# Summing two modulation rows over partitions by accumulating and doubling transfers

## The chip, the cores and the metric

The kernel runs on one core of a Trainium2 chip. TensorE (PE) multiplies matrices, VectorE (DVE) and ScalarE (ACT) do elementwise work, GpSimd (POOL) and SyncE (SP) mostly issue transfers (DMAs), and 16 DMA engines move the data. On-chip memory (SBUF) and the matrix accumulators (PSUM) have 128 partitions. The metric is the time of one execution in microseconds (us), lower is better; the kernel before takes 1791.58 us, the median of three runs (1788.38, 1791.58, 1792.2).

## The reference

One decoder layer, x of 256 tokens by 2048 channels in float32, modulated by a conditioning vector c of 2048. What matters here:

```python
mod = (silu(c) @ w_ada + b_ada).reshape(B, 6, 1, D)
sh1, sc1, gt1, sh2, sc2, gt2 = (mod[:, j] for j in range(6))
h = rmsnorm(x, g_mix) * (1 + sc1) + sh1
z = h @ w_in                       # three token mixers and three gates come from z
...
merged = (sigmoid(gm) * (out_m @ w_branch[0]) + sigmoid(gd) * (out_d @ w_branch[1])
          + sigmoid(gs) * (out_s @ w_branch[2]))
x = x + gt1 * (merged @ w_out)
h = rmsnorm(x, g_ffn) * (1 + sc2) + sh2
hid = h @ w_up
gate = causal_dwconv(hid[..., :D_FF], w_ffconv)
x = x + gt2 * ((silu(gate) * hid[..., D_FF:]) @ w_down)
```

The two gates gt1 and gt2 are rows of 2048 numbers. In the kernel tokens lie on partitions where a gate is used, so each gate is wanted as a tile of 128 partitions that all hold the same row.

## The kernel before

**Products.** All large products go through `gemm` (line 350). It walks the inner dimension in steps of four 128-row tiles. For each step `weights` (line 330) loads 1 MB from SP into one of three `raw` buffers, ACT casts two tiles at a time to the rounded type (`hi`, line 342), DVE subtracts to get the remainder (`lo`, line 344; four buffers each for `hi` and `lo`), and PE multiplies hi and lo parts (lines 377 and 391) into PSUM banks; three banks carry the tag `gp`.

**Modulation rows beside the products.** The rows of `mod` are not made on PE. `ada_late` (line 286) makes 512 columns, called a group here, in eight steps: each loads 512 KB of `w_ada` from SP into one of three `ada` buffers (line 293) and DVE multiplies by a column of silu(c) and adds into an accumulator `acc` (two instructions a step, lines 222 and 224). At the end `acc` holds 128 partial sums, one on each partition. There are two `acc` buffers.

**Gate rows.** `ada_row` (line 308) does four such groups. After each it loads 512 numbers of the bias from POOL (`br`, line 315), adds them to partition 0 of `acc` (line 316), splits `acc` into hi and lo parts (ACT line 418, DVE line 419), multiplies both by a 128x128 matrix of ones (two PE instructions into `pr`, line 321), which leaves the sum over partitions on every partition, and copies it to the row (ACT, line 322).

**Order.** The steps stand as a Python generator in the queue `ada`. `tick()` (line 209) is called after each four-tile step of a product and advances that queue by `rates["ada"]` steps on average: the source weaves the modulation steps among the products with these rates. `issue_after` holds an instruction behind another one on the same engine. A planner then sets each engine's order when the program is built: it walks a timing model of its own and issues what that model has ready. On the chip every queue runs in that order and an instruction that waits holds up those behind it.

**Where the two rows stand.** The row for `gt1` is appended at line 962 ahead of `branch(0, ...)`, at 1.4 steps per tick; what is left is drained at line 967. Then POOL loads the two halves of x again (`x2`, line 970), and the product with `w_out` uses the row in line 981. The row for `gt2` is appended at line 1045, in the second chunk of the up product, at 0.8 steps per tick; it is first used in line 1083, after the first down product.

Of the kernel before, what the change touches and what calls it, by code (L numbers as in the profile page):

```python
# [10 lines left out]
F32 = mybir.dt.float32  # L11
F32R = mybir.dt.float32r
AF = mybir.ActivationFunctionType
ALU = mybir.AluOpType
# [3 lines left out]
P = 128  # L18
# [21 lines left out]
def kernel(  # L40
# [6 lines left out]
    nc = tc.nc  # L47
# [7 lines left out]
    adap = ctx.enter_context(tc.tile_pool(name="adap", bufs=3))  # L55
# [5 lines left out]
    adaps = ctx.enter_context(tc.tile_pool(name="adaps", bufs=1, space=PSUM))  # L61

    def slot(i, name):
        n = NT * MH * (MDH + 1) + 8 if i == 2 else 2048
        return slots.tile([P, n], F32, tag=f"s{i}", name=name)
# [13 lines left out]
    V, A, T = nc.vector, nc.scalar, nc.tensor  # L79
# [6 lines left out]
    ones_r = const.tile([P, P], F32R, name="ones_r")  # L86
# [105 lines left out]
    ada = deque()  # L192
# [14 lines left out]
    rates = {"ada": 0.0, "side": 1.0}  # L207
# [9 lines left out]
    def ada_mac(accs, raw, kt0, nk):  # L217
        for k in range(nk):
# [4 lines left out]
            else:  # L223
                state["mac"] = V.scalar_tensor_tensor(acc, raw[:, k, :], ccol[:, kt:kt + 1], acc, ALU.mult, ALU.add)  # L224

    def partition_sums(acc):

        pm = adaps.tile([P, 512], F32, tag="adaps", name="pm")
        for k in range(4):
            T.transpose(pm[:, k * P:(k + 1) * P], acc[:, k * P:(k + 1) * P], ident)  # L230
        sums = tmp.tile([P, 4], F32, tag="sums", name="sums")
        V.tensor_reduce(sums, pm.rearrange("p (k f) -> p k f", k=4), AX.X, ALU.add)
        return sums
# [52 lines left out]
    def ada_late(comp, g):  # L286

        acc = adap.tile([P, 512], F32, tag="acc", name="acc", bufs=2)
        c0 = comp * D + g * 512
        for q in range(8):  # L290
            raw = adap.tile([P, 2, 512], F32, tag="ada", name="araw")
            with tc.issue_after(state["load"].ins):
                nc.sync.dma_start(raw, w_ada[q * 256:(q + 1) * 256, c0:c0 + 512].rearrange("(k p) f -> p k f", p=P))
            with tc.issue_after(state["split"].ins):
                ada_mac([acc], raw, 2 * q, 2)
            yield acc

    def ada_columns(comp, bcol, dst, gcol=None):
        for g in range(4):
            for acc in ada_late(comp, g):  # L300
                yield
            pm = partition_sums(acc)
            ks = slice(4 * g, 4 * g + 4)
            V.tensor_tensor(dst[:, ks], pm[:, 0:4], bcol[:, ks], ALU.add)
            if gcol is not None:
                V.tensor_tensor(dst[:, ks], dst[:, ks], gcol[:, ks], ALU.mult)

    def ada_row(comp, dst):

        for g in range(4):  # L310
            for acc in ada_late(comp, g):
                yield
            br = adap.tile([P, 2, 512], F32, tag="ada", name="br")[:, 0, :]
            c0 = comp * D + g * 512
            nc.gpsimd.dma_start(br[0:1, :], b_ada[0:1, c0:c0 + 512])
            V.tensor_tensor(acc[0:1, :], acc[0:1, :], br[0:1, :], ALU.add)
            pr = adaps.tile([P, 512], F32, tag="adaps", name="pr")
            parts = adap.tile([P, 2, 512], F32R, tag="ada", name="parts")
            split(parts[:, 0, :], parts[:, 1, :], acc)
            for i in range(2):  # L320
                T.matmul(pr, lhsT=ones_r, rhs=parts[:, i, :], start=i == 0, stop=i == 1)  # L321
            A.copy(dst[:, g * 512:(g + 1) * 512], pr)

    a1 = const.tile([P, KD], F32, name="a1")
    b1 = const.tile([P, KD], F32, name="b1")
# [90 lines left out]
    def split(hi, lo, src):  # L416

        A.copy(hi, src)
        return V.tensor_tensor(lo, src, hi.bitcast(F32), ALU.subtract)
# [438 lines left out]
    def branch(bi, col_g, act, order):  # L858
        for ch in range(4):
            if order == 0:  # L860
                sg = mg_of(ch)
            else:
                sg = [wide("sg"), wide("sg")]
                gates(col_g, ch, sg)
            accb = gemm("T", act, w_branch[bi], 0, ch * 512, 512, 0, KM)
            for tt in range(NT):
                d = mg_of(ch)[tt]
                V.tensor_tensor(sg[tt], accb[tt], sg[tt], ALU.mult)
                if order:
                    V.tensor_tensor(d, d, sg[tt], ALU.add)  # L870
            if order == 2:
                for k2 in range(2):
                    pb = bank("pmg")
                    for tt in range(NT):
                        for j in range(2):
                            k = 2 * k2 + j
                            T.transpose(pb[:, j * S + tt * P:j * S + (tt + 1) * P], mg_of(ch)[tt][:, k * P:(k + 1) * P],
                                        ident)
                    h0 = (ch % 2) * 4 + 2 * k2
                    split(mgh[ch // 2][:, h0:h0 + 2, :], mgl[ch // 2][:, h0:h0 + 2, :],  # L880
                          pb.rearrange("p (a t) -> p a t", a=2))
            tick()
# [31 lines left out]
    for ch in range(2):  # L914
        acc = gemm("T", hact, w_in, 0, C_MO + ch * 512, 512, 0, KD)
# [6 lines left out]
    for ch in range(2):  # L922
        acc = gemm("T", hact, w_in, 0, C_MV + ch * 512, 512, 0, KD)
# [5 lines left out]
    for t, col0, f0 in ((mqT, C_MQ, 0), (mkT, C_MK, 8)):  # L929
        for ch in range(2):  # L930
            acc = gemm("H", h1act, w_in, 0, col0 + ch * 512, 512, 0, KD)
# [28 lines left out]
    mgl = [slots.tile([P, 8, S], F32R, tag=f"s{i}", name=f"mgl{i}") for i in (6, 7)]  # L960
    gt1 = slot(0, "gt1")
    ada.append(ada_row(2, gt1))
    rates["ada"] = 1.4
    branch(0, C_GM, mlstm.out, 2)


# [9 lines left out]
    for ch in range(4):  # L976
        acc = gemm("T", mact, w_out, 0, ch * 512, 512, 0, KD)
# [57 lines left out]


    gt2 = slot(8, "gt2")
    rates["ada"] = 0.8
    NCH = DFF // 512
    for half, (c0, c1) in enumerate(((0, 6), (6, NCH))):  # L1040
        ath = [slots.tile([P, 8, S], F32R, tag=f"s{i}", name=f"ath{i}") for i in (0, 3, 4)]
        atl = [slots.tile([P, 8, S], F32R, tag=f"s{i}", name=f"atl{i}") for i in (5, 6, 7)]
        for ch in range(c0, c1):
            if ch == 1:
                ada.append(ada_row(5, gt2))
# [19 lines left out]
            i, j0 = (ch - c0) // 2, ((ch - c0) % 2) * 4  # L1065
# [12 lines left out]
        for n in range(4):  # L1078
            acc = gemm("T", act, w_down, c0 * 512, n * 512, 512, 0, 4 * (c1 - c0))
# [37 lines left out]
```

## Time and profile before

| | before |
|---|---|
| median of three runs | 1791.58 us |
| the profiled execution, its own time | 1787.35 us |
| span of that execution | 1785.6 us |
| granted PE clock | 0.999 of full |
| busy: PE / DVE / ACT / POOL | 99% / 73% / 53% / 1% |
| products with ones of the two rows (line 321) | 16 |
| transfers issued from POOL for the two rows (line 315) | 8 |

A profile page has the share of each engine, the span in 40 slices, the chain of work that ended last (followed back from the last instruction to what released each step), and groups of instructions with busy time, mean duration and what ended the idle time before them. Further views used below list one engine's instructions in order of time, who waited for whom, the busy times in chosen windows, and the DMAs with the time from issue to landing. In a window row the columns after the window are its length, then busy us (and instructions) of PE, PE's weight loads, DVE, ACT and POOL, then the granted PE clock, the share of the DMA engines that was busy, and GB/s. PE's busy share counts overlapping instructions once, so how fast PE runs is better read from the distance between starts.

### The profile page before, as it was taken

How to read it: one execution, taken by the hardware profiler on the slowest of the kernel's cores; microseconds unless marked ns; L12 is line 12 of the kernel's file. 1: busy time of each engine (PE TensorE's matmuls, PEld its weight loads, DVE VectorE, ACT ScalarE, POOL GpSimd, SP SyncE). 2: the span in 40 equal slices, each digit the busy share in tenths (PEclk: the TensorE clock that was granted, in tenths of full speed). 3: DMA queues.
4: the chain of work that ended last, by engine and by line, in shares of the span. 5: the costliest groups of instructions: out<-in, count | busy, mean ns of one | idle time of the engine just before them, and what ended most of it. 6: DMA issues, size and time to landing. Idle time of an engine off the chain costs nothing.

```text
span 1785.6 us, 23761 instructions
## 1 busy us (share of the span) xinstructions
PE 1762.2 (99%) x9168; PEld 1512.5 (85%) x9168; DVE 1302.4 (73%) x1734; ACT 951.9 (53%) x1338; POOL 16.4 (1%) x44
## 2 busy tenths in 40 slices
PE   7899999999999999999999999999999999999998
PEld 6898999888878887888888888888888888888887
DVE  6887646878888778777996577888875556666654
ACT  6667655666565556544444555555553345555432
POOL 2000000000000000000000000000000000000000
PEclk9999999999999999999999999999999999999999
DMA  9999855776777567778896547777755555555563
GB/s 338 346 330 313 289 179 178 266 244 242 248 238 259 200 216 251 240 261 294 308 323 216 181 166 259 253 251 267 268 204 198 193 189 189 189 189 189 189 214 117
DMA packets 219731, 423.33 MB, mean 237 GB/s; under 512 B 9027, under 2 KB 31675, under 8 KB 219105
## 3 DMA queue, kind: packets, MB, share of 16 engines
q1 hardware_dynamic: 217328, 417.44, 68.8%
q0 software_dynamic: 1008, 2.23, 0.4%
q10 hardware_dynamic: 1280, 2.14, 0.3%
q8 instruction: 72, 1.18, 0.3%
q14 instruction: 43, 0.34, 0.1%
HBM read 419.68 MB, written 2.10 MB: 236 GB/s over the span
## 4 chain that ended last, share of the span: by engine, by line
PE 95%; ACT 2%; DMA 1%; DVE 1%; issue 1%; SPq 0%; ACTq 0%
PE gp L391 55%; PE acch L377 32%; PE kept L396 2%; PE gp L396 2%; DMA raw<-in_w_in_dram 1%; ACT hi L342 1%; PE psc L679 0%; PE pm L240 0%; DMA x<-in_x_dram 0%; DVE quads L224 0%; PE spin L186 0%; ACT x L444 0%; PE pr L321 0%; PE pxt L453 0%; PE ptf L739 0%
## 5 line engine op out<-in xcount | busy, mean ns | idle before, releaser
L344 DVE TENSOR_TENSOR lo<-raw,hi 128x1024 fp32r<-128x1024 f32 (+1 forms) x608 | 724.0, 1208 | 363.4 <-ACT hi L342 327.1
L342 ACT CAST hi<-raw 128x1024 fp32r<-128x1024 f32 (+1 forms) x608 | 617.6, 1039 | 552.4 <-PE gp L391 353.6
L391 PE MATMUL gp<-hi,h 128*128 128x512 f32 (+1 forms) x1600 | 411.4, 387 | 7.0 <-ACT hi L342 5.7
L377 PE MATMUL acch<-h,hi 128*128 128x512 f32 x1664 | 403.3, 392 | 0.2 <-DVE h L1032 0.2
L377 PEld LDWEIGHTS acch<-h,hi 128*128 128x128 f32 x1664 | 303.6, 188 | 58.0 <-DVE h L1032 1.1
L391 PEld LDWEIGHTS gp<-hi,h 128*128 128x128 f32 x1600 | 295.7, 188 | 60.7 <-ACT hi L342 8.8
L391 PE MATMUL gp<-lo,h 128*128 128x512 f32 (+1 forms) x800 | 227.5, 384 | 0.0
L377 PEld LDWEIGHTS acch<-h,lo 128*128 128x128 f32 x1664 | 217.8, 191 | 11.1
L377 PE MATMUL acch<-h,lo 128*128 128x256 f32 x1664 | 221.3, 283 | 0.0
L224 DVE SCALAR_TENSOR_TENSOR acc<-araw,ccol,acc 128x512 f32<-128x512 f32 x240 | 179.3, 748 | 6.0 <-DMA araw<-in_w_ada_dram 4.3
L391 PEld LDWEIGHTS gp<-lo,h 128*128 128x128 f32 x800 | 149.7, 188 | 26.2 <-DVE lo L344 0.8
L391 PE MATMUL gp<-hi,atl 128*128 128x512 f32 x352 | 137.2, 390 | 0.0
L391 PE MATMUL gp<-hi,ath 128*128 128x512 f32 x352 | 136.9, 389 | 0.0
L391 PE MATMUL gp<-lo,ath 128*128 128x512 f32 x352 | 105.9, 390 | 0.0
L391 PEld LDWEIGHTS gp<-hi,atl 128*128 128x128 f32 x352 | 66.1, 188 | 13.7
L391 PEld LDWEIGHTS gp<-hi,ath 128*128 128x128 f32 x352 | 66.1, 188 | 13.7
L391 PEld LDWEIGHTS gp<-lo,ath 128*128 128x128 f32 x352 | 66.1, 188 | 13.6
L224 DVE SCALAR_TENSOR_TENSOR quads<-raw,ccol,quads 128x1024 f32<-128x1024 f32 x45 | 57.7, 1282 | 2.8 <-DMA raw<-in_w_ada_dram 2.2
L391 PE MATMUL gp<-hi,mgl 128*128 128x512 f32 x128 | 50.4, 394 | 0.0
L391 PE MATMUL gp<-hi,mgh 128*128 128x512 f32 x128 | 50.0, 392 | 0.0
L1057 DVE SCALAR_TENSOR_TENSOR y<-gsum,cols,y 128x255 f32<-128x255 f32 (+1 forms) x88 | 41.4, 479 | 3.7 <-ACT y L1055 3.5
L391 PE MATMUL gp<-lo,mgh 128*128 128x512 f32 x128 | 38.3, 391 | 0.0
(365 smaller groups left out, 1601.2 us busy)
## 6 DMA issues: line engine op xcount, KB each, us to landing
raw<-in_w_in_dram SPq DMA_DIRECT2D x98, 1024.0 KB, 5.1
raw<-in_w_up_dram SPq DMA_DIRECT2D x88, 1024.0 KB, 5.1
araw<-in_w_ada_dram SPq DMA_DIRECT2D x128, 512.0 KB, 5.9
raw<-in_w_down_dram SPq DMA_DIRECT2D x44, 1024.0 KB, 5.1
raw<-in_w_ada_dram SPq DMA_DIRECT2D x62, 512.0 KB, 5.9
raw<-in_w_branch_dram SPq DMA_DIRECT2D x24, 1024.0 KB, 5.1
raw<-in_w_in_dram SPq DMA_DIRECT2D x25, 880.0 KB, 5.0
raw<-in_w_out_dram SPq DMA_DIRECT2D x16, 1024.0 KB, 5.0
```

Source lines behind the costliest of these rows:

```text
L224: state["mac"] = V.scalar_tensor_tensor(acc, raw[:, k, :], ccol[:, kt:kt + 1], acc, ALU.mult, ALU.add)
L342: A.copy(hi[:, :, :n], raw[:, k0:k0 + 2, :n])
L344: state["split"] = V.tensor_tensor(lo[:, :, :n], raw[:, k0:k0 + 2, :n], hi[:, :, :n].bitcast(F32), ALU.subtract)
L377: T.matmul(acc[t][:, 0:m], lhsT=w[k // 2][:, k % 2, sl], rhs=ah(s0 + k)[:, 0:m], start=start, stop=s0 + k == kt1 - 1 and w is (wh if flip ...
L391: T.matmul(o, lhsT=a(s0 + k)[:, sl], rhs=wk[:, :n], **kw)
L396: T.matmul(o, lhsT=wk[:, sl], rhs=a(s0 + k), **kw)
L1057: V.scalar_tensor_tensor(yf[:, sft:S], src[:, 0:S - sft], wc(2 - sft), yf[:, sft:S], ALU.mult, ALU.add)
```

## The change

In `ada_row` the products with ones go. In each group `fold(acc)` sums over partitions in place: seven transfers from POOL, each adding the upper half of what is left onto the lower half (64, 32, 16, 8, 4, 2 and 1 partitions of 2 KB). Then the bias is added to partition 0 as before, and one more transfer copies the 2 KB to partition 0 of the row. After the four groups seven transfers double the row (1, 2, 4, ... 64 partitions of 8 KB) until all 128 partitions hold it. The steps per tick go from 1.4 to 2.0 for the first row and from 0.8 to 1.1 for the second.

```diff
+    def fold(acc):
+
+        n = P // 2
+        while n:
+            nc.gpsimd.dma_start(acc[0:n], acc[n:2 * n], accum_op=ALU.add)
+            n //= 2
+
...
         for g in range(4):
             for acc in ada_late(comp, g):
                 yield
+            fold(acc)
             br = adap.tile([P, 2, 512], F32, tag="ada", name="br")[:, 0, :]
             c0 = comp * D + g * 512
             nc.gpsimd.dma_start(br[0:1, :], b_ada[0:1, c0:c0 + 512])
             V.tensor_tensor(acc[0:1, :], acc[0:1, :], br[0:1, :], ALU.add)
-            pr = adaps.tile([P, 512], F32, tag="adaps", name="pr")
-            parts = adap.tile([P, 2, 512], F32R, tag="ada", name="parts")
-            split(parts[:, 0, :], parts[:, 1, :], acc)
-            for i in range(2):
-                T.matmul(pr, lhsT=ones_r, rhs=parts[:, i, :], start=i == 0, stop=i == 1)
-            A.copy(dst[:, g * 512:(g + 1) * 512], pr)
+            nc.gpsimd.dma_start(dst[0:1, g * 512:(g + 1) * 512], acc[0:1, :])
+        n = 1
+        while n < P:
+            nc.gpsimd.dma_start(dst[n:2 * n, :], dst[0:n, :])
+            n *= 2
...
     ada.append(ada_row(2, gt1))
-    rates["ada"] = 1.4
+    rates["ada"] = 2.0
     branch(0, C_GM, mlstm.out, 2)
...
     gt2 = slot(8, "gt2")
-    rates["ada"] = 0.8
+    rates["ada"] = 1.1
```

## The prediction

> **What bounds the kernel now.** I read the page's shares and chain first, then the stage of the first row (813 to 973 us).
>
> ```profile
> span 1785.6 us, 23761 instructions
> PE 1762.2 (99%) x9168; PEld 1512.5 (85%) x9168; DVE 1302.4 (73%) x1734; ACT 951.9 (53%) x1338; POOL 16.4 (1%) x44
> PE 95%; ACT 2%; DMA 1%; DVE 1%; issue 1%; SPq 0%; ACTq 0%
> ```
>
> PE carries 95% of the chain that ended last: an instruction fewer on PE is time saved as long as the others feed it. For the window 800 to 980 us that chain is PE alone:
>
> ```profile
> by line: PE gp L391 96.7%; PE pmg L877 1.9%; PE pr L321 1.0%; PE px L1005 0.2%; PE pm L230 0.2%
> ```
>
> How near the others are shows in the windows:
>
> ```profile
> 872.00:904.00 32.00, 32.00 (x146) 26.45 (x145) 29.05 (x36) 14.05 (x17) 0.48 (x1) 1.00 0.93 324
> 940.00:960.00 20.00, 20.00 (x94) 16.55 (x93) 13.20 (x14) 9.21 (x12) 0.57 (x1) 1.00 0.70 246
> 1140.00:1180.00 40.00, 40.00 (x234) 35.44 (x233) 34.43 (x48) 20.32 (x29) 0.00 (x0) 1.00 0.79 273
> ```
>
> While the first row is made, DVE is busy 91% and the DMA engines 93%; once it is done they fall to 66% and 70%. The second row's stage (third line) has 86% and 79%.
>
> **What goes from PE.** The distance between starts gives PE's pace:
>
> ```profile
> 855.31 0.62 PE L321 MATMUL pr<-parts,ones_r 128*128 128x512 f32 x2
> 855.77 1.09 PE L391 MATMUL gp<-hi,h 128*128 128x512 f32 x4
> L321 PE MATMUL pr<-parts,ones_r x16: 392/394/396, 855.3 to 1319.3; 128*128 128x512 f32 x16
> ```
>
> Two products take 0.46 us of PE's order, so 0.23 each (the 394 ns of one overlap its neighbours). Sixteen: 16 x 0.23 = 3.7 us, all on the chain. First term: -3.7.
>
> The splits (lines 418 and 419) and the copy (322) of eight groups leave ACT and DVE, neither of which is on this chain: nothing by themselves.
>
> **How long the new path is.** No row shows a transfer from on-chip memory to itself, nor one that adds. The nearest are these (KB each, median us from issue to landing; below, POOL's issue time and the spread of landings):
>
> ```profile
> rows<-in_c_dram SPq DMA_DIRECT2D x1, 8.0 KB, 1.6
> x2a<-in_x_dram POOLq DMA_DIRECT2D x1, 1024.0 KB, 5.0
> br<-in_b_ada_dram POOLq DMA_DIRECT2D x8, 2.0 KB, 4.3
> L315 POOL DMA_DIRECT2D br<-in_b_ada_dram x8: 484/484/512, 836.9 to 1294.1; - x8
> DMA to landing us min/median/max: 3.2/4.3/6.7
> ```
>
> Call one step of the new chains s. It lies between 1.6 (SP, almost idle engines) and 6.7. I take 3.2, the shortest `br`: same queue, same busy engines, but the source lies on chip; its end for the range is 4.3 and beyond. The Trainium skill, "DMA: Bandwidth & Descriptors" (Anatomy of one DMA), fits 2.0 us plus bytes over 436 GB/s for a POOL transfer, which would be an estimate of 2.0 to 3.2 us a step here and make every wait below vanish. This trace's 2 KB took 3.2 to 6.7, so the rows decide.
>
> A group's chain c is seven folds, the bias add and the copy to the row: 8s plus one add.
>
> ```profile
> L316 DVE TENSOR_TENSOR acc<-acc,br x8: 673/679/681, 842.2 to 1311.2; 1x512 f32<-1x512 f32 x8
> ```
>
> c = 8s + 0.7. The doubling d is seven steps that grow to 512 KB; at most 0.7 each above a small one (5.0 against 4.3), I take half: d = 7s + 2.5.
>
> **When the first row is there.** Its first multiply, two of its bias loads (one group apart), and its deadline:
>
> ```profile
> 813.21 0.48 DVE L222 TENSOR_SCALAR acc<-araw,ccol 128x512 f32<-128x512 f32 x1
> 902.05 0.48 POOL L315 DMA_DIRECT2D br<-in_b_ada_dram  x1 [31.61 <-PE gp L391]
> 934.03 0.48 POOL L315 DMA_DIRECT2D br<-in_b_ada_dram  x1 [31.50 <-DVE acc L224]
> L981 DVE TENSOR_TENSOR t<-gp,gt x8: 682/691/692, 972.4 to 1043.4; 128x512 f32<-128x512 f32 x8
> ```
>
> A group of eight steps at 1.4 a tick takes 32 us, so a tick is 32 x 1.4 / 8 = 5.6 us; at 2.0 a group takes 22.5. The first ends near 813.2 + 22.5 = 835.7. The later ones go slower, since `br` keeps one of the three `ada` buffers until its add, which now waits for the folds, 7s. With two buffers left and
>
> ```profile
> araw<-in_w_ada_dram SPq DMA_DIRECT2D x128, 512.0 KB, 5.9
> L224 DVE SCALAR_TENSOR_TENSOR acc<-araw,ccol,acc 128x512 f32<-128x512 f32 x240 | 179.3, 748 | 6.0 <-DMA araw<-in_w_ada_dram 4.3
> ```
>
> a step takes (5.9 + 1.5) / 2 = 3.7 us instead of 2.8. At s = 3.2 that holds for 23 us, some 6 steps, and the other two take 5 us: a group of 28. (The two `acc` buffers ask for less: c = 26.3.) The multiplies end at 835.7 + 3 x 28 = 920, the last chain at 946, the row at 971, just ahead of 972.4. By the same working s = 2.5 gives 957 and s = 4.3 gives 835.7 + 3 x 29.6 + 35.1 + 32.6 = 992. The point from which it is late is about s = 3.3. I cost it at nothing; without that cover each us late is one for PE.
>
> POOL's order: behind the new transfers in the source stand the two x loads.
>
> ```profile
> 739.45 0.58 POOL L970 DMA_DIRECT2D x2b<-in_x_dram  x1 [179.75 <-ACT num L819]
> 952.18 0.57 POOL L970 DMA_DIRECT2D x2a<-in_x_dram  x1 [17.67 <-PE gp L391]
> ```
>
> One is issued before the row begins; the other waits for PE's last use of its place. Behind the last doubling it would be issued at about 968 and land 5.0 later, with the row. Nothing beyond the row's own lateness.
>
> **The second row.** Its first multiply, and its deadline:
>
> ```profile
> 1090.05 0.48 DVE L222 TENSOR_SCALAR acc<-araw,ccol 128x512 f32<-128x512 f32 x1
> L1083 DVE TENSOR_TENSOR t<-gp,gt x16: 681/691/692, 1348.3 to 1780.6; 128x512 f32<-128x512 f32 x16
> ```
>
> With the same tick a group is 8 / 1.1 x 5.6 = 41 us, the multiplies end near 1254, the row at 1257 + 15s = 1305, 43 us early; late only from s = 6.1. Nothing.
>
> **What the higher rate costs.** At 2.0 steps a tick needs 1.05 MB of weights and 1.05 MB of `w_ada`: 2.10 MB in 5.6 us is 374 GB/s. The window of 872 moved 324 at a share of 0.93, so 348 with nothing idle: a tick becomes 6.0 us, short by 0.4 in each of 16 ticks, 6.5 us. DVE needs, from the same window, 29.05 less 16 x 0.75 and the removed split, 16.3 in 5.7 ticks, 2.9 a tick; with four multiply-adds 5.9 against 5.6, short by 5 us in 16 ticks. What covers this:
>
> ```profile
> ACT hi L342 <- PE gp L391: 77.7, 48, 3.4
> ```
>
> From 800 to 980 us ACT waited 48 times for a `hi` buffer that PE frees: conversions run ahead until the four buffers are full, three spare ones of twelve products at 0.23, some 8 us. Both shortfalls fit in, and the shortage of `ada` buffers eases both. In SP's order more `w_ada` loads stand ahead of each weight load, and one that waits for its buffer holds the weights behind it, again under that cover. Bounds 0 (these are waits, no gain) to 6.5; I take +2, since other waits use the cover too.
>
> **The new wait on DVE.** The bias add now stands behind seven folds, and behind it in DVE's order stand the `lo` splits that PE needs. Where the planner put such an add:
>
> ```profile
> 937.38 1.53 DVE L224 SCALAR_TENSOR_TENSOR acc<-araw,ccol,acc 128x512 f32<-128x512 f32 x2
> 940.83 0.68 DVE L316 TENSOR_TENSOR acc<-acc,br 1x512 f32<-1x512 f32 x1 [1.92 <-DMA br<-in_b_ada_dram]
> 941.44 1.21 DVE L344 TENSOR_TENSOR lo<-raw,hi 128x1024 fp32r<-128x1024 f32 x1
> ```
>
> The load issued at 934.03 landed 6.7 later, and DVE stood for 1.92 with a split behind it, so real waits are not foreseen exactly. But the planner does move work: x2b, written after the row in the source, was issued ahead of it. I expect the add late in DVE's order, off by under 1 us a step, 7 us a group, against 8 us of cover, thinner in the first stage. Bounds 0 (a wait gains nothing) to 8 x (7 x 2 - 8) = 48, off by 2 a step (5.2 for the 3.2 taken, inside the rows); I take +3, near the low end, as one `br` wait in eight is the nearest row.
>
> **Sum.** -3.7 + 2 + 3 = +1.3 on the profiled execution's 1787.35 (span 1785.6, 1.75 around it): 1788.65. The median is 4.2 above that execution, which gives 1791.58 + 1.3 = 1793 as runs are timed. A measurement of this kernel tells about 0.2%, 3.6 us, from no change.
>
> **Rivals.** A, the first row is late: line 981 waits for it, and with two of three banks unread PE stops after about 1.4 us of products. From s = 3.3 on; at 3.8 the row is some 10 us late, 9 more than the forecast, 1802; at the median of the `br` loads, 4.3, 20 late, 1812. For it: half of those loads took 4.3 or more, and the forecast has 1 us to spare. Against: their source is HBM. Chance 0.28.
>
> B, the planner takes a fold for shorter than it is by more than 1.2 us. DVE then stands at each of eight adds beyond PE's cover. At 1.7 off, 8 x (12 - 8) = 32 replaces the +3: 1822. For it: the 1.92 above. Against: one wait in eight. Chance 0.16.
>
> C, all is hidden: 1791.6 - 3.7 = 1788, from 3.5 to 5 under before if the pace elsewhere is a little better. For it: PE waits nowhere in 800 to 980 us though DVE and DMA are over 90%. Against: it needs every cover at once. Chance 0.22, of which 0.16 beyond 0.2%.
>
> D, a rule of the chip: each POOL issue waits for the DVE instruction under way, about 0.75 to 1.2 us of a multiply-add or split. That makes s 4.2, the row 18 us late: 1810. Against: eight issues at 484 to 512 ns while DVE was busy about 90%. Chance 0.04. The rule is that of the Trainium skill, "SBUF — State Buffer" (Who interferes with whom): DVE in its two-port modes shuts GpSimd out of the port with which it writes transfer descriptors. The trace does not show it.
>
> **Numbers.** Forecast 0.30, all within 0.2%. Slower: A + B + D = 0.48; same: 0.30 + 0.06 = 0.36; faster 0.16. Cases of both signs hold much, so the forecast's own range stands here: 1789 to 1795. Range: low 1785, C less 3 us for the spread of runs (3.8 before); high 1822, B, which takes in A up to 4.3; left out are worse forms of A and B.
>
> **What would show it.** PE without line 321; the group chains 26 us, from the first fold's issue to the copy's landing; adds (line 316) with DVE idle under 8 us before them and no PE wait behind them; the row landing just ahead of 972 and line 981 waiting for PE. Wrong if line 981 or the adds wait for DMA and PE's starts open behind them, or if steps take 4 us or more.

## The result and the profile after

The changed kernel takes 1843.53 us (median of four runs, 1840.54 to 1846.33) against 1790.47 us in the runs of the kernel before on the same chip: a ratio of 1.0298, 95% interval [1.0283, 1.0313], 53 us slower. That is outside the predicted range of 1785 to 1822. One execution of kernel 10 below took 4674 us, for a reason that is not known, and is left out of its ratio.

The first lines of the page after (span; busy time and share of each engine):

```profile
span 1839.6 us, 23854 instructions
PE 1773.4 (96%) x9152; PEld 1515.6 (82%) x9152; DVE 1295.7 (70%) x1726; ACT 941.7 (51%) x1322; POOL 72.0 (4%) x122
```

PE has its 16 products fewer (9152 against 9168) and is busy 11.2 us longer. The other part is idle: span less busy is 66.2 us where it was 23.4. 42.8 + 11.2 = 54.0, the whole difference of the two spans.

Where PE stood, from the view of waits (us in total, times, longest), and what DVE, which it waited for, waited for in turn:

```profile
PE gp L398 <- DVE t L988: 14.5, 1, 14.5
PE acch L384 <- DVE lo L351: 12.3, 6, 8.5
PE gp L398 <- DVE lo L351: 10.4, 5, 5.4
```

```profile
DVE acc L324 <- DMA acc<-acc: 27.7, 6, 11.3
DVE acc L324 <- issue: 13.2, 2, 8.9
DVE t L988 <- DMA gt<-gt: 17.2, 1, 17.2
```

The lines are those of the changed file: 324 is the bias add (316 before), 988 the first use of the first row (981), 351 the `lo` split. There are two troubles. DVE stood 40.9 us in all at the eight bias adds, and PE ran out of split weights behind it (22.7 us). ("issue" means that the view names no releaser; these two adds, at 1209.53 and 1254.56, began 4.2 and 2.2 us after POOL had issued the last fold of their group, so the chain is the likely releaser there too.) And the first row came late: DVE stood 17.2 us at line 988 and PE 14.5.

Both show in DVE's order of time near the end of the first row:

```profile
969.42 0.69 DVE L877 TENSOR_TENSOR mg<-mg,sg 128x512 f32<-128x512 f32 x1
981.39 0.68 DVE L324 TENSOR_TENSOR acc<-acc,br 1x512 f32<-1x512 f32 x1 [11.29 <-DMA acc<-acc]
982.00 2.34 DVE L351 TENSOR_TENSOR lo<-raw,hi 128x1024 fp32r<-128x1024 f32 x2
...
1014.35 1.29 DVE L988 TENSOR_TENSOR t<-gp,gt 128x512 f32<-128x512 f32 x2 [17.19 <-DMA gt<-gt]
```

An add of one partition keeps DVE 11.29 us, and two splits that PE wants stand right behind it. The chain itself, on POOL, for the first group (the start of the fold, its second and last step, then the copy):

```profile
840.16 0.89 POOL L230 DMA_DIRECT2D acc<-acc  x1 [5.60 <-PE gp L398]
847.74 0.78 POOL L230 DMA_DIRECT2D acc<-acc  x1 [6.69 <-DMA acc<-acc]
...
873.59 0.77 POOL L230 DMA_DIRECT2D acc<-acc  x1 [2.01 <-DMA acc<-acc]
...
879.55 0.52 POOL L325 DMA_DIRECT2D gt<-acc  x1 [2.38 <-DVE acc L324]
```

From the first fold to the seventh are six steps in 33.4 us, 5.6 each. The step was put at 3.2. In the fourth group, behind the last loads of `w_ada`, the steps are shorter, (977.50 - 956.39) / 6 = 3.5, with less traffic on the DMA engines (the value before the last, here for the first and the fourth group):

```profile
956.39 0.82 POOL L230 DMA_DIRECT2D acc<-acc  x1 [1.42 <-DVE acc L224]
...
977.50 0.81 POOL L230 DMA_DIRECT2D acc<-acc  x1 [0.89 <-DMA acc<-acc]
```

```profile
836.00:876.00 40.00, 40.00 (x182) 33.01 (x181) 30.96 (x39) 18.06 (x21) 6.10 (x8) 1.00 0.87 284
956.00:980.00 24.00, 23.67 (x109) 19.24 (x107) 11.33 (x13) 10.02 (x12) 6.60 (x9) 1.00 0.73 237
```

The extra busy time of PE is a slower clock behind its longer stops. PE's order of time around one (start, duration):

```profile
979.05 0.39 PE L398 MATMUL gp<-hi,mgh 128*128 128x512 f32 x1
979.28 0.39 PE L398 MATMUL gp<-hi,mgl 128*128 128x512 f32 x1
983.26 0.90 PE L398 MATMUL gp<-lo,mgh 128*128 128x512 f32 x2 [3.60 <-DVE lo L351]
983.96 0.63 PE L398 MATMUL gp<-hi,mgh 128*128 128x512 f32 x1
984.39 0.63 PE L398 MATMUL gp<-hi,mgl 128*128 128x512 f32 x1
984.82 0.63 PE L398 MATMUL gp<-hi,mgh 128*128 128x512 f32 x1
```

Ahead of the gap of 3.60 us starts are 0.23 apart, behind it 0.43, and by 987 they are at 0.23 again. The granted clock in the windows (third value from the end, before DMA share and GB/s) says the same:

```profile
860.00:880.00 20.00, 20.00 (x92) 16.46 (x91) 15.09 (x18) 9.39 (x12) 4.14 (x6) 1.00 0.82 270
900.00:920.00 20.00, 14.04 (x50) 10.63 (x49) 11.41 (x15) 5.42 (x6) 2.67 (x5) 0.83 0.65 218
1000.00:1020.00 20.00, 5.50 (x15) 4.03 (x14) 3.71 (x5) 2.46 (x6) 1.52 (x3) 0.60 0.33 82
```

In the window of 860 PE never stops and has its full clock; in the windows of 900 and 1000, where it stops once for 5.4 us and once for 14.5, the mean falls to 0.83 and 0.60. 11.2 us more busy time with 3.7 us of products removed makes about 15 us of slow clock, an estimate.

### The profile page after: what moved, and what is told of

The parts are those of the page before. It is cut to its first block, busy times and chain, and to the rows that moved or that the text cites. A ratio compares the mean times of both kernels' runs of the same rounds, so it can differ in the third digit from the quotient of the medians.

```text
span 1839.6 us, 23854 instructions
## 1 busy us (share of the span) xinstructions
PE 1773.4 (96%) x9152; PEld 1515.6 (82%) x9152; DVE 1295.7 (70%) x1726; ACT 941.7 (51%) x1322; POOL 72.0 (4%) x122
## 5 line engine op out<-in xcount | busy, mean ns | idle before, releaser
L398 PE MATMUL gp<-hi,mgh 128*128 128x512 f32 x128 | 52.1, 407 | 14.5 <-DVE t L988 14.5
L230 POOL DMA_DIRECT2D acc<-acc x56 | 44.2, 789 | 253.4 <-DMA acc<-acc 189.2
```

Source lines behind the costliest of these rows:

```text
L230: nc.gpsimd.dma_start(acc[0:n], acc[n:2 * n], accum_op=ALU.add)
L398: T.matmul(o, lhsT=a(s0 + k)[:, sl], rhs=wk[:, :n], **kw)
```

## The experiments

Kernel 1 is that of experiment 1, and so on. Ratios are against runs of the kernel before on the same chip, with 95% intervals. The changed kernel ran on other occasions than these, so what a kernel gains over it goes by the difference of the two ratios. Theory W says that the loss comes from the two waits, because a step of a chain takes 5 to 6 us.

**1. The rates alone.** The kernel before with

```diff
-    rates["ada"] = 1.4
+    rates["ada"] = 2.0
...
-    rates["ada"] = 0.8
+    rates["ada"] = 1.1
```

> The kernel before with only the rates of the change (2.0 and 1.1 steps per tick), products with ones kept. Theory W (waits): the 53 us come from DVE standing at the eight bias adds and at line 981 for the late row, because a chain step takes 5 to 6 us; then rates alone cost what the prediction put at +2, so 1788 to 1797. Rival C (crowding): the higher rate starves the products of loads and DVE time; then most of the 53 us is here already, 1810 or more.

Measured: 1788.59 us, ratio 0.9992 [0.9982, 1.0001]. The higher rates cost nothing that can be measured; crowding is out.

**2. The transfers beside the products.** On top of kernel 1, for the first row (`beside` copies `acc[0:1]` into `scr` and issues the seven adding folds on `scr`):

```diff
+            if comp == 2:
+                if g == 0:
+                    scr = sidewide("scr")
+                    nc.gpsimd.memset(scr, 0.0)
+                beside(scr, acc)
...
+        n = 1 if comp == 2 else P
+        while n < P:
+            nc.gpsimd.dma_start(scr[n:2 * n, :], scr[0:n, :])
+            n *= 2
```

> As the rates-only kernel, and for the first row the same transfers are issued from POOL on a scratch tile of 128x512 (copy of one partition, seven adding folds for each group, then seven doublings of 2 KB rows, a quarter of the bytes), and nothing waits for them. Theory W: within 4 us of the rates-only kernel. Rival T (traffic): the transfers themselves slow loads and engines; then 10 us or more above it.

Measured: 1790.57 us, ratio 1.0011 [1.0001, 1.0020], 2 us above kernel 1. The first row's folds, with nobody waiting, are almost free, though they take 5.7 us a step here too (first group, 851.11 to 885.28). The first row's traffic is out up to those 2 us; its doublings moved a quarter of the bytes, and the second row's transfers were not tried this way.

**3. The bias ahead of the folds.**

```diff
-            fold(acc)
             br = adap.tile([P, 2, 512], F32, tag="ada", name="br")[:, 0, :]
             c0 = comp * D + g * 512
             nc.gpsimd.dma_start(br[0:1, :], b_ada[0:1, c0:c0 + 512])
             V.tensor_tensor(acc[0:1, :], acc[0:1, :], br[0:1, :], ALU.add)
+            fold(acc)
```

> The changed kernel with the bias added to partition 0 ahead of the folds, so that DVE no longer waits behind a chain; the sum is the same. Theory W: the PE waits behind the adds (some 25 us) and the slower clock after them go, the late first row stays: 1805 to 1822. If the adds cost little and the late row is all: above 1835.

Measured: 1812.05 us, ratio 1.0122 [1.0106, 1.0139], 31 us less than the changed kernel. What is left is mainly the late row; its waits on PE and DVE are longer than in the changed kernel, 20.3 for 14.5 and 23.0 for 17.2:

```profile
PE gp L398 <- DVE t L988: 20.3, 1, 20.3
...
PE gp L398 <- DVE lo L351: 1.0, 1, 1.0
```

```profile
DVE t L988 <- DMA gt<-gt: 23.0, 1, 23.0
```

PE's other wait for DVE, the splits, has shrunk from 22.7 us to 1.0, and PE is busy 1763.5 us in place of 1773.4: some 10 us of the slow clock hung on the adds.

**4. One spread in place of the doublings.** The row is gathered in device memory:

```diff
+        row = dramp.tile([1, D], F32, tag="row", name="row")
...
-            nc.gpsimd.dma_start(dst[0:1, g * 512:(g + 1) * 512], acc[0:1, :])
-        n = 1
-        while n < P:
-            nc.gpsimd.dma_start(dst[n:2 * n, :], dst[0:n, :])
-            n *= 2
+            nc.gpsimd.dma_start(row[0:1, g * 512:(g + 1) * 512], acc[0:1, :])
+        nc.gpsimd.dma_start(dst, row.broadcast_to([P, D]))
```

> The changed kernel with the seven doublings replaced by one transfer: the row is gathered in device memory and read back with all 128 partitions at once; the folds and the adds behind them stay. The first row is there about 20 us earlier. Theory W: line 981's wait of 17 us and the slow clock behind it go, the adds stay: 1815 to 1830. If lateness of the row costs little: above 1838.

Measured: 1824.17 us, ratio 1.0199 [1.0181, 1.0218], 18 us less than the changed kernel. Nothing waits at the row's first use any more. Now the splits are PE's wait and the adds DVE's:

```profile
PE acch L383 <- DVE lo L350: 12.2, 5, 8.9
PE gp L397 <- DVE lo L350: 9.5, 4, 4.2
```

```profile
DVE acc L326 <- DMA acc<-acc: 40.9, 7, 11.9
```

Kernels 3 and 4 each leave the wait that they did not touch.

**5. Both.** Kernels 3 and 4 together.

> Bias ahead of the folds and one transfer in place of the doublings, rates 2.0 and 1.1: both waits are taken away while the folds stay. Theory W: all of the loss is gone and the 3.7 us of the products remain as a gain, less up to 4 us for the rates: 1786 to 1792. If a third cost is in the change: 1800 or more.

Measured: 1796.41 us, ratio 1.0052 [1.0035, 1.0069]: the expectation was too good by some 4 us. The two gains do not quite add up: 0.0052, some 9 us, is left. The row is still late (PE stands 5.3 us behind its first use), and an accumulator that its chain holds stops DVE once:

```profile
DVE t L987 <- DMA gt<-row: 10.6, 1, 10.6
...
DVE acc L223 <- DMA acc<-acc: 6.6, 1, 6.6
```

These are the chain's length again, at the row's end and at the two `acc` buffers; that no third cost hides in these 9 us is argued here, and kernels 9 and 10, with the waits gone, leave no room for one.

**6 and 7. One row at a time.** In each kernel one of the two calls uses the old `ada_row` with its old rate.

> Only the first row by transfers (rate 2.0), the second by products with ones as before (rate 0.8). In the trace of the changed kernel the shift against before grows by 35 us at the first row and 16 at the second. Theory W: 1822 to 1832. If one row's loss hangs on the other's, the two one-row kernels do not add up to 53 us.

> Only the second row by transfers (rate 1.1), the first by products with ones as before (rate 1.4). Theory W: its row is in time, so only the four adds cost: 1802 to 1812.

Measured: the first row alone 1823.62 us, ratio 1.0197 [1.0182, 1.0212], 35.5 us; the second alone 1805.11 us, ratio 1.0098 [1.0083, 1.0112], 16.9 us. Together 52.4 of the 53 us: the rows add up. The second row has only the adds, and PE's wait for splits is its one large wait:

```profile
PE acch L400 <- DVE lo L367: 11.4, 5, 8.4
```

**8. The step by itself.** A kernel without the layer, one execution, with chains of `dma_start` alone as in `fold` and in the doubling, once quiet and once beside this stream:

```python
for i in range(110):
    k0, c0 = (i % 4) * 512, (i // 4) * 512
    nc.sync.dma_start(raws[i % 3], w_in[0, k0:k0 + 512, c0:c0 + 512].rearrange("(k p) f -> p k f", p=P))
```

> No layer is computed: chains of transfers alone, first with idle DMA engines, then beside a stream of 1 MB loads from SP. Seven adding folds from POOL, the same seven as plain copies from POOL and from ACT, seven doublings of 8 KB rows from POOL and from ACT. If the load stream makes a step long: quiet adding step under 3 us, loaded 5 to 6, copies alike. If adding makes it long: adding step 4 us or more when quiet, plain copies 2 to 2.5.

POOL's order of time, first and last of seven adding folds and of seven plain copies, quiet and then beside the loads:

```profile
5.86 0.97 POOL L59 DMA_DIRECT2D acc<-acc  x1 [5.41 <-DMA acc<-in_x_dram]
...
21.71 0.78 POOL L59 DMA_DIRECT2D acc<-acc  x1 [1.50 <-DMA acc<-acc]
24.49 0.57 POOL L65 DMA_DIRECT2D acc<-acc  x1 [2.00 <-DVE acc L76]
...
37.00 0.51 POOL L65 DMA_DIRECT2D acc<-acc  x1 [1.35 <-DMA acc<-acc]
...
98.43 0.83 POOL L59 DMA_DIRECT2D acc<-acc  x1 [27.57 <-DVE raw L89]
...
133.16 0.78 POOL L59 DMA_DIRECT2D acc<-acc  x1 [4.57 <-DMA acc<-acc]
139.32 0.57 POOL L65 DMA_DIRECT2D acc<-acc  x1 [5.38 <-DVE acc L76]
...
171.32 0.51 POOL L65 DMA_DIRECT2D acc<-acc  x1 [4.61 <-DMA acc<-acc]
```

Six steps each: adding 15.85 / 6 = 2.6 us quiet and 34.7 / 6 = 5.8 loaded; plain 2.1 quiet and 5.3 loaded. The load stream makes the step long, adding puts half a us on it. The same plain chain from ACT's queue, each time in one line from the first issue to the end of the seventh:

```profile
39.22 12.50 ACTq L65 DMA_DIRECT2D acc<-acc  x7
...
207.15 37.78 ACTq L65 DMA_DIRECT2D acc<-acc  x7
```

The seventh issue is at 51.16 and at 244.34, so its six steps are 2.0 quiet and 6.2 loaded; of the loaded ones the first took 11.4 (the second issue is at 218.51) and the other five 5.2 each. Beside the loads that is no shorter than from POOL: the issuing queue is not the cause. The stream fills the DMA engines more (share 1.04) than the layer does (0.87 in the first group).

**9 and 10. Fold once.** The multiply-adds write into the row's tile, so one chain serves all four groups, and the bias comes by an adding transfer:

```diff
-            for acc in ada_late(comp, g):
+            for acc in ada_late(comp, g, dst[:, g * 512:(g + 1) * 512]):
                 yield
...
+        nc.gpsimd.dma_start(dst[0:1, :], b_ada[0:1, comp * D:(comp + 1) * D], accum_op=ALU.add)
+        fold(dst)
+        nc.gpsimd.dma_start(row, dst[0:1, :])
+        nc.gpsimd.dma_start(dst, row.broadcast_to([P, D]))
```

> The multiply-adds go straight into the row's own tile, so the four groups are folded together: per row one adding transfer brings the bias from device memory, seven folds of 8 KB rows, one copy out and one spread to all partitions, 10 in place of 43; no DVE add, no accumulator held by a chain. Rates 2.0 and 1.1. Theory W: at 5 to 7 us a step the first row's chain is some 60 us after its multiplies end near 905, so it is there near 965, just in time; nothing waits, and 1785 to 1790. If the first row is late by a few us: 1790 to 1797. If a cost of the folds is still unexplained: above 1797.

> The same with 2.4 steps per tick for the first row, so that it is there about 10 us earlier if the loads keep up. Theory W: 1785 to 1789, at or below the one at 2.0. If the loads do not keep up at 2.4 (2.3 MB in 5.6 us is 410 GB/s), the products stop for weights: 1790 to 1800.

Measured: at 2.0 steps 1787.45 us, ratio 0.9989 [0.9981, 0.9998]; at 2.4 steps 1784.86 us, ratio 0.9983 [0.9974, 0.9993], some 3 us below the kernel before. Both intervals end below 1, but both gains are smaller than the 0.2% that the prediction took as the least to be told from no change, and between the two the intervals overlap. In the first, DVE still waits a little for the row,

```profile
DVE t L985 <- DMA gt<-row: 3.7, 1, 3.7
```

and in the second not at all: its spread leaves at 959.80 and line 985 begins at 971.2, waiting for PE.

```profile
959.80 0.58 POOL L326 DMA_DIRECT2D gt<-row  x1 [3.27 <-PE gp L395]
```

```profile
L985 DVE TENSOR_TENSOR t<-gp,gt x8: 680/691/692, 971.2 to 1042.1; 128x512 f32<-128x512 f32 x8
```

## Why the prediction was wrong

**The step of the chain, the failed step.** The term that was mis-sized is s, one step of a chain. The prediction took 3.2 us, the shortest `br`, "same queue, same busy engines, but the source lies on chip". Measured: 5.6 in the first group, and in kernel 8 an on-chip plain step of 2.1 quiet and 5.3 beside loads. That the source lies on chip saves nothing that can be seen; how full the DMA engines are decides. The nearest row was taken from the wrong end: with DMA shares of 0.8 to 0.9 the longest `br`, 6.7, was nearer than the shortest. The late row, which 3.2 put at nothing, and the wait at the adds, which it put at 3 us, are the loss. The Trainium skill, "DMA: Bandwidth & Descriptors" (Anatomy of one DMA), has 2.0 us and bytes over 436 GB/s; kernel 8's quiet plain step of 2.1 agrees with it, the loaded one is 2.5 times as long.

**The group chain** was put at 26 us; from 840.16 to the issue of the copy at 879.55 it is already 39. **The row** was put at 971; it was there at 1014, 42 us late by the first use of before, and later than rival A's 992. The step accounts for most of that: with 5.6 the prediction's own sum gives 835.7 + 3 x 29.6 + 45.5 + 41.7 = 1012. DVE's stops at the adds moved the row by little, for in kernel 3, without them, it is there at 1007.71:

```profile
1007.71 1.29 DVE L988 TENSOR_TENSOR t<-gp,gt 128x512 f32<-128x512 f32 x2 [23.01 <-DMA gt<-gt]
```

That the sum lands so near is luck in its parts. The multiplies end at 956, where it has 925, and the last chain and the doublings, beside fewer loads, are shorter than it has them. What it misses is that the two `acc` buffers, set aside because they "ask for less", set the pace at this step: the third group's first multiply stands at 884.55, just behind the first group's chain, and in kernel 3 the wait for that chain shows as 7.0 us.

**The adds.** The prediction has them "off by under 1 us a step, 7 us a group, against 8 us of cover", +3 in all. DVE stood up to 11.3 us, and kernel 3 puts the price at 31 us. So the mechanism was named, the size chosen at the low end. That rival B has 32 is luck: it lets DVE stand 12 us at each of eight adds, with 8 of them covered. DVE stood 40.9 / 8 = 5.1 on average; PE stopped 22.7 us all the same, so the cover was thinner, and the slow clock behind these stops came on top.

**One out of two.** Forecast and rivals let either the row be late (A, 0.28) or the adds wait (B, 0.16). Both hang on the same step, so both came: 31 us and 18 us, together 49 of 53 when each is taken away alone (both together took away 44). A range made from separate cases left out the case in which one number fails them all.

**What held.** Sixteen products seem worth about what was said: in kernel 10, with the waits gone, the gain is 0.0017 x 1789 = 3.0 us (interval 1.3 to 4.7) where 3.7 was forecast, and PE is busy 1759.1 us where it was 1762.2. No run takes the products out alone, so this is agreement and no proof. The rates were given +2 and cost nothing (0.9992). The second row was in time: with its last doubling issued at 1371.48 it stood ready some 24 us before its first use at 1402.2, where 43 were forecast; in kernel 7, where nothing delays that use but its own adds, the two are at 1336.38 and 1361.6.

```profile
1371.48 0.52 POOL L328 DMA_DIRECT2D gt<-gt  x1 [6.39 <-DMA gt<-gt]
```

Rival D, DVE shutting POOL out, did not show: a fold's issue keeps POOL 0.75 to 0.89 us in the changed kernel and 0.76 to 0.97 in kernel 8, where DVE is all but idle, and in kernel 8 the loaded fold takes 5.8 us a step while DVE is busy 0.54 us in 41,

```profile
98.00:139.00 41.00, 0.54 (x2) 5.51 (x7) 1.00 1.04 366
```

and the stream of loads fills the DMA engines (here the columns are the length, then DVE and POOL busy, clock, DMA share and GB/s).

**What was left out.** The slow clock behind the longer stops, about 15 us by the estimate above, was in no term: a us of waiting was priced as a us.

## What to carry to other kernels

A chain of dependent small transfers costs its number of steps times the latency under the load that is there, not the quiet one, and bytes count for less (kernel 8's loaded doublings went from 5.3 us at 8 KB to 7.8 at 256 KB): cut steps (one fold for four groups, one spread in place of seven doublings) before anything else. Never put an instruction that waits for such a chain into the order of an engine that feeds the bound engine; here moving the add of each group ahead of its chain was worth 31 us. When several costs hang on one unknown number, price the case in which it is at its bad end for all of them together.

## What the runs showed of the hardware that was not expected

In kernel 8 a dependent on-chip transfer of 128 KB down to 4 KB took 2.1 us from POOL with idle DMA engines and 5.3 beside a stream of 1 MB loads, and from ACT 2.0 and, behind a first one of 11.4, 5.2; adding into the destination made it 2.6 and 5.8. In the changed kernel, behind a gap of 3.6 us PE ran at half pace, 0.43 in place of 0.23 us a product, for about 3.7 us. The Trainium skill, "TensorE: Matmul & The Clock Gate" (Part 1: The HAM clock gate), says that about 3.4 us of idling halve the clock and that about as much busy time restores it; the trace agrees.
